# Small tiles in a pool of their own, and TensorE's dense operands at multiples of 256 bytes

## The chip, the cores and the metric

One core of a Trainium2 chip runs the whole program. The metric is the device time of one execution in microseconds, the median of several runs. TensorE multiplies, VectorE (DVE) and ScalarE (ACT) work on elements, GpSimd (POOL) does little here, and SyncE (SP) issues nearly all DMA transfers.

## The reference

Two layers of a decoder work on x of 1024 rows by 1024 columns, float32. Each layer does two things, and normalises the rows before and after each of them.

1. Mixing: h = norm(x) times a scale plus a shift, both from the condition vector c; one projection of h gives queries (8 heads of 64), keys and values (2 heads), and 512 columns u. Queries attend to the 128 last positions, with a sink for each head; u goes through trailing means of 2, 4, 8 and 16 rows and a small matrix for each group. The two results, 512 columns each, go through an output projection, are normalised, gated and added to x.
2. Feed-forward: f = (silu(h Wg) * (h Wu)) Wd with an inner width of 2816, then normalised, gated and added to x.

```
proj = h @ w_in + b_in;  q, k, v, u = split(proj)
x = x + gate_m * norm(concat(attention(q, k, v), pool(u)) @ w_out)
h = norm(x) * (1 + scale_f) + shift_f
x = x + gate_f * norm((silu(h @ w_gate) * (h @ w_up)) @ w_down)
```

## The kernel before

The 1024 rows are two halves of 512. To keep float32 accuracy every operand is split in two parts, hi and lo (`split`, lines 210 and 211: ScalarE rounds to float32r, VectorE subtracts), and every product is three matmuls (`mm3`, lines 236, 239 and 240): hi by hi, moving lo by stationary hi, moving hi by stationary lo, all into one PSUM bank. In the first argument after the destination stands the stationary operand, 128 columns; the other one moves, 512 columns in the dense stages, and each matmul loads its stationary operand anew.

The dense stages of each layer, in their order:
- `q_pass`, `kv_pass`, `u_pass`: the input projection. Weights come to `raw` tiles and are split into `hi` and `lo`; the activations stand split in `hT`. In the first two hT is stationary, in u_pass it moves. kv_pass moves 256 columns.
- `natural_proj`: the output projection; both operands are split into `hi` and `lo` tiles.
- `up_firsts`, `up_pair`: gate and up products, in seven products by a Strassen-like scheme (`double`, 8 groups of three matmuls for each right-hand operand into two banks). Stationary are weights in hi and lo; moving are `hT` in the first products and, after the region "up" is made, `t1`, `t2`, `t3`, `t4` and `b22`.
- `down`: seven products over 22 groups of inner columns. Stationary are activations in hi and lo; moving are weights in `bh`, with `ph` or `bl` for their low part, and in the last product `one_` and `two_` tiles.

Between the projections run the attention (scores with stationary `qT` and moving keys in `sa`; values with stationary `vz` and moving `pth` and `ph`; 256 columns each) and transposes, in which the identity `ident` moves and the transposed tile is stationary. Streams of work are Python generators that are stepped in turn, so the order of instructions is fixed by the code; the tile framework adds waits where tiles depend on each other. PSUM has four banks `acc` for dense products.

Memory: tiles lie in pools one behind the other, and `t_` takes a tile by its name from the pool that has it. The pool `const` begins at byte 16512 of each partition and holds 3840 bytes, with `ident` first; `sb` begins at 20352 and holds 126592 bytes, with small tiles (statistics, columns, rows, halos) between the large ones; the regions "mix", "up" and "down" follow at 146944, one after the other in the same place. In the trace the numbers at the end of tile names are left out: t stands for t1 to t4, b for b22, two_b and one_b for the tiles two_... and one_....

Addresses modulo 256 (of the first byte in a partition; slices of 128 or 512 columns begin at multiples of 512 bytes behind it):

| tiles | before |
|---|---|
| ident | 128 |
| raw, hi, lo, hT, fn, ar, sa, sb | 192 |
| G, ada, ph | 128 |
| t1 to t4, b22, bh, bl, one_, two_ | 0 |
| qT, vz, pth in layer 0 | 128 |
| qT, vz, pth in layer 1 | 0 |

Of the kernel before, what the change touches and what calls it, by code (L numbers as in the profile page):

```python
# [11 lines left out]
F32 = mybir.dt.float32  # L12
F32R = mybir.dt.float32r
# [7 lines left out]
P = 128  # L21
# [16 lines left out]
KD = D // P  # L38
# [27 lines left out]
def hybrid_decoder_kernel(  # L66
# [22 lines left out]
    nc = tc.nc  # L89

    const = ctx.enter_context(tc.tile_pool(name="const", bufs=1))
    sb = ctx.enter_context(tc.tile_pool(name="sb", bufs=1))
    ps = ctx.enter_context(tc.tile_pool(name="ps", bufs=1, space=PSUM))
    dr = ctx.enter_context(tc.tile_pool(name="dr", bufs=1, space=DRAM))


    SHARED = dict(
        hT=8, fn=4, raw=2, hi=3, lo=3, sa=2, sb=2, ar=2, ada=1, ph=3,
        junk=1, st=12, rs=8, ss=4, halo=8, G=1, rows=1, cols=2, colp=4, sk=2,
    )  # L100
    REGIONS = dict(
        mix=dict(cfa=2, cfb=2, qkv=6, bqkv=1, uT=4, pt=2, vz=5, rt=1, qT=1, pth=2, pwh=1, pwl=1),
        up=dict(t2=8, t1=8, t3=8, b22=8, t4=8),
# [8 lines left out]
            now.update(name=name, pool=tc.alloc_tile_pool(name=name, bufs=1, reuse_waits="tile"))  # L112

    def t_(tag, shape, dt=F32):
        if tag in SHARED:
            return sb.tile(shape, dt, tag=tag, name=tag, bufs=SHARED[tag])
        return now["pool"].tile(shape, dt, tag=tag, name=tag, bufs=REGIONS[now["name"]][tag])
# [3 lines left out]
    def part(tag, n=512):  # L121

        tile_, used = now.get(tag, (None, WIDE[tag]))
        if used + n > WIDE[tag]:
            tile_, used = t_(tag, [P, WIDE[tag]], F32 if tag == "raw" else F32R), 0
        now[tag] = (tile_, used + n)
        return tile_[:, used : used + n]
# [8 lines left out]


    eye = t_("G", [P, D])[:, :P]
    make_identity(nc, eye)
    ident_r = const.tile([P, P], F32R, name="ident")  # L140
    nc.vector.tensor_copy(ident_r, eye)
    ident = ident_r.bitcast(F32)
    ones = t_("pt", [P, P])
    nc.vector.memset(ones, 1.0)
    ones_r = const.tile([P, 1], F32R, name="ones_r")
    nc.vector.tensor_copy(ones_r, ones[:, 0:1])
    ones = ones_r.bitcast(F32)
    pick_row = t_("rt", [P, 7])
    nc.vector.memset(pick_row, 0.0)
    nc.vector.memset(pick_row[:, 3:4], 1.0)  # L150
    picks = const.tile([P, 7], F32R, name="picks")
    nc.vector.tensor_copy(picks, pick_row)

    mask = const.tile([P, 2, 2 * P], F32, name="mask")
# [18 lines left out]
    nc.vector.reciprocal(rcnt, rcnt)  # L173


    c_raw = const.tile([P, KD], F32, name="c_raw")
    nc.sync.dma_start(c_raw, c[0].rearrange("(p j) -> p j", j=KD))
    c_act = const.tile([P, KD], F32, name="c_act")
    nc.scalar.activation(c_act, c_raw, AF.Silu)


# [230 lines left out]
    def load_gate(l, sub):  # L412
        G = t_("G", [P, D])
        nc.sync.dma_start(G, gates[l, sub].to_broadcast([P, D]))
        return G
# [504 lines left out]
    def mix_out(l, cats, G):  # L920
        order = [*range(GRP, KD), *range(GRP)]
        left = [cats[k // 4][:, k % 4, :] for k in order]

        def wsrc(i, nh):
            k = order[i]
            cs = slice(nh * 512, (nh + 1) * 512)
            if k < GRP:
                return (
                    (slice(0, HD), None, w_out[l, k * HD : (k + 1) * HD, cs]),
                    (slice(HD, P), None, w_out[l, (GRP + k) * HD : (GRP + k + 1) * HD, cs]),  # L930
                )
            return ((ALLP, None, w_out[l, k * P : (k + 1) * P, cs]),)

        fn = [t_("fn", [P, D]) for _ in range(NT)]
        ss = t_("ss", [P, 8])
        return fn, ss, natural_proj(fn, left, wsrc, ss, G)
# [373 lines left out]
    for l in range(DEPTH):  # L1310
        cols = par["cols"]
# [37 lines left out]
        G = load_gate(l, 0)  # L1349
        fn, ss, out0 = mix_out(l, cats[0], G)  # L1350
# [23 lines left out]
        fn, ss, out1 = mix_out(l, cats[1], G)  # L1374
# [38 lines left out]
        G = load_gate(l, 1)  # L1413
# [3 lines left out]
        fn = [[t_(tag, [P, D]) for _ in range(NT)] for tag in ("fn",)]  # L1417
        fn.append([t_(tag, [P, D]) for tag in ("sa", "sa", "sb", "sb")])
        ss = [t_("ss", [P, 8]) for _ in range(NHALF)]
# [53 lines left out]
def build(arrays):  # L1473
    import concourse.bacc as _bacc

    nc = _bacc.Bacc("TRN2", target_bir_lowering=False, num_devices=1)
    args = []
    for name in _INS:
        a = arrays[f"in_{name}_dram"]
        args.append(  # L1480
            nc.dram_tensor(f"in_{name}_dram", a.shape, mybir.dt.from_np(a.dtype), kind="ExternalInput").ap()
        )
    for i, (shape, dtype) in enumerate(_OUTS):
        dt = mybir.dt.from_np(np.dtype(dtype))
        args.append(nc.dram_tensor(f"out_{i}_dram", shape, dt, kind="ExternalOutput").ap())
    with tile.TileContext(nc) as tc:
        hybrid_decoder_kernel(tc, *args)
    return nc
# [9 lines left out]
```

## Time and profile before

| | |
|---|---|
| median of 3 runs | 1985.68 us (1984.56 to 1991.52) |
| profiled execution | 1988.62 us |
| its span, first to last instruction | 1986.8 us |
| granted TensorE clock over the span | 0.988 |
| TensorE matmuls busy | 96%, 8958 instructions |
| weight loads busy | 78%, 8958 instructions |
| VectorE busy | 79%, 2907 instructions |
| ScalarE busy | 48%, 1794 instructions |
| GpSimd busy | 3%, 100 instructions |
| DMA | 336.62 MB, 169 GB/s over the span |

A busy time is the union of an engine's instructions. Matmuls are pipelined: one starts before the last one's end, so that how long one lasts in the rows is not how far it moves the next one; the starts in the timeline tell that.

### The profile page before, as it was taken

The numbers are of one execution on the slowest core, as the hardware profiler recorded it, in microseconds if no ns is written. First come the engines' busy times: TensorE is split into PE (matmuls) and PEld (weight loads), VectorE is DVE, ScalarE is ACT, GpSimd is POOL, SyncE is SP. The second block draws the span as 40 slices with busy tenths as digits, with TensorE's granted clock in tenths as the row PEclk, the third lists the DMA queues.
The fourth block names the chain that finished last, engine by engine and source line by source line (L and its number), as shares of the span: only waits on it lengthen the run. The fifth ranks groups of instructions, "written<-read, shape, count | busy, mean of one in ns | idle before, by whom it ended". The sixth has DMA issues, their size and how long they took to land. (4 is left out here: it accounts for less than half of the span.)

```text
span 1986.8 us, 26045 instructions
## 1 busy us (share of the span) xinstructions
PE 1898.7 (96%) x8958; PEld 1548.8 (78%) x8958; DVE 1566.9 (79%) x2907; ACT 957.0 (48%) x1794; POOL 50.3 (3%) x100
## 2 busy tenths in 40 slices
PE   7989989999999999999999899899999999999997
PEld 4777778877888887778887778788788788878886
DVE  6888975778888886877878889656887888667687
ACT  4775775662222223445648658745622222234452
POOL 1000000020000000000000000000200000000000
PEclk9999999999999999999999899999999999999999
DMA  9336554556455556833565455446555554474343
GB/s 325 87 118 191 184 167 133 174 181 198 162 169 175 165 165 243 280 123 101 169 201 174 128 149 186 137 129 191 170 185 175 188 174 157 153 259 156 112 138 106
DMA packets 222052, 336.62 MB, mean 169 GB/s; under 512 B 16696, under 2 KB 120008, under 8 KB 221920
## 3 DMA queue, kind: packets, MB, share of 16 engines
q1 hardware_dynamic: 221776, 334.92, 51.7%
q8 instruction: 70, 1.15, 0.2%
q14 instruction: 62, 0.51, 0.1%
q0 software_dynamic: 32, 0.00, 0.0%
q10 hardware_dynamic: 112, 0.04, 0.0%
HBM read 262.00 MB, written 72.89 MB: 169 GB/s over the span
## 5 line engine op out<-in xcount | busy, mean ns | idle before, releaser
L210 ACT ACTIVATE hi<-raw 128x1024 fp32r<-128x1024 f32 (+1 forms) x388 | 331.9, 867 | 341.1 <-PE acc L239 224.5
L211 DVE TENSOR_TENSOR lo<-raw,hi 128x1024 fp32r<-128x1024 f32 (+1 forms) x388 | 381.2, 988 | 82.5 <-ACT hi L210 82.2
L236 PE MATMUL acc<-t,hi 128*128 128x512 f32 x704 | 277.0, 393 | 5.1 <-ACT hi L210 5.1
L240 PE MATMUL acc<-t,lo 128*128 128x512 f32 x704 | 276.5, 394 | 5.0 <-DVE lo L211 5.0
L239 PE MATMUL acc<-t,hi 128*128 128x512 f32 x704 | 277.1, 394 | 0.0
L236 PE MATMUL acc<-bh,hi 128*128 128x512 f32 x528 | 205.5, 394 | 3.0 <-ACT bh L210 3.0
L240 PE MATMUL acc<-bh,lo 128*128 128x512 f32 x528 | 208.2, 394 | 0.0
L236 PE MATMUL acc<-hT,hi 128*128 128x512 f32 x480 | 192.0, 400 | 10.6 <-ACT hi L210 10.0
L1058 DVE TENSOR_TENSOR fn<-acc,fn 128x512 f32<-128x512 f32 x220 | 150.7, 685 | 53.1 <-PE acc L240 52.0
L239 PE MATMUL acc<-hT,hi 128*128 128x512 f32 x480 | 189.7, 395 | 0.0
L240 PE MATMUL acc<-hT,lo 128*128 128x512 f32 x480 | 188.2, 394 | 0.0
L240 PEld LDWEIGHTS acc<-t,lo 128*128 128x128 f32 x704 | 133.0, 189 | 36.9 <-DVE lo L211 7.9
L236 PEld LDWEIGHTS acc<-t,hi 128*128 128x128 f32 x704 | 132.9, 189 | 36.2 <-ACT hi L210 6.9
L239 PEld LDWEIGHTS acc<-t,hi 128*128 128x128 f32 x704 | 132.9, 189 | 28.9
L239 PE MATMUL acc<-ph,hi 128*128 128x512 f32 x320 | 127.4, 398 | 1.1 <-DVE ph L211 1.1
L236 PEld LDWEIGHTS acc<-bh,hi 128*128 128x128 f32 x528 | 99.1, 188 | 26.5 <-ACT bh L210 3.8
L270 DVE SCALAR_TENSOR_TENSOR ada<-ar,c_act,ada 128x512 f32<-128x512 f32 x140 | 104.6, 747 | 18.1 <-DMA ar<-in_ada_w_dram 16.8
L240 PEld LDWEIGHTS acc<-bh,lo 128*128 128x128 f32 x528 | 100.0, 189 | 22.6
L236 PEld LDWEIGHTS acc<-hT,hi 128*128 128x128 f32 x480 | 91.2, 190 | 30.5 <-ACT hi L210 11.4
L996 ACT ACTIVATE fn<-fn 128x512 f32<-128x512 f32 x44 | 27.9, 633 | 170.6 <-DVE fn L1058 170.6
L240 PEld LDWEIGHTS acc<-hT,lo 128*128 128x128 f32 x480 | 90.9, 190 | 18.8 <-DVE lo L211 0.4
L239 PEld LDWEIGHTS acc<-hT,hi 128*128 128x128 f32 x480 | 91.6, 191 | 17.6
(302 smaller groups left out, 3877.4 us busy)
## 6 DMA issues: line engine op xcount, KB each, us to landing
ar<-in_ada_w_dram SPq DMA_DIRECT2D x160, 256.0 KB
raw<-in_w_gate_dram SPq DMA_DIRECT2D x44, 512.0 KB
raw<-in_w_up_dram SPq DMA_DIRECT2D x44, 512.0 KB
raw<-in_w_in_dram SPq DMA_DIRECT2D x80, 256.0 KB
raw<-keeps SPq DMA_DIRECT2D x40, 512.0 KB
keeps<-fn SPq DMA_DIRECT2D x66, 256.0 KB
two_b<-in_w_down_dram SPq DMA_DIRECT2D x30, 512.0 KB
raw<-keepa SPq DMA_DIRECT2D x25, 512.0 KB
```

The source lines that it names most:

```text
L210: nc.scalar.activation(hi, src, AF.Copy)
L211: nc.vector.tensor_sub(lo, src, hi.bitcast(F32))
L236: ins = nc.tensor.matmul(dst, lh, rh, start=first, stop=False)
L239: nc.tensor.matmul(dst, lh, rl, start=False, stop=False)
L240: return nc.tensor.matmul(dst, ll, rh, start=False, stop=last)
L270: nc.vector.scalar_tensor_tensor(acc, w, c_act[:, i : i + 1], acc, op0=ALU.mult, op1=ALU.add)
L996: nc.scalar.activation(g, g, AF.Silu)
L1058: nc.vector.tensor_add(halves_of(dst)[m], bank, halves_of(src)[m])
```

## The change

The tiles of few bytes (junk, st, rs, ss, halo, rows, cols, colp, sk) leave the pool `sb` for a pool `small` that is opened before it. In `const` four small tiles are allocated ahead of `ident`. No operation, shape or buffer count is another.

```diff
     const = ctx.enter_context(tc.tile_pool(name="const", bufs=1))
+    small = ctx.enter_context(tc.tile_pool(name="small", bufs=1))
     sb = ctx.enter_context(tc.tile_pool(name="sb", bufs=1))
...
-    SHARED = dict(
-        hT=8, fn=4, raw=2, hi=3, lo=3, sa=2, sb=2, ar=2, ada=1, ph=3,
-        junk=1, st=12, rs=8, ss=4, halo=8, G=1, rows=1, cols=2, colp=4, sk=2,
-    )
+    SMALL = dict(junk=1, st=12, rs=8, ss=4, halo=8, rows=1, cols=2, colp=4, sk=2)
+    SHARED = dict(hT=8, fn=4, raw=2, hi=3, lo=3, sa=2, sb=2, ar=2, ada=1, ph=3, G=1)
...
     def t_(tag, shape, dt=F32):
+        if tag in SMALL:
+            return small.tile(shape, dt, tag=tag, name=tag, bufs=SMALL[tag])
         if tag in SHARED:
...
+    ones_r = const.tile([P, 1], F32R, name="ones_r")
+    picks = const.tile([P, 7], F32R, name="picks")
+    c_raw = const.tile([P, KD], F32, name="c_raw")
+    c_act = const.tile([P, KD], F32, name="c_act")
     ident_r = const.tile([P, P], F32R, name="ident")
...
-    ones_r = const.tile([P, 1], F32R, name="ones_r")
...
-    picks = const.tile([P, 7], F32R, name="picks")
...
-    c_raw = const.tile([P, KD], F32, name="c_raw")
...
-    c_act = const.tile([P, KD], F32, name="c_act")
```

By the sizes of the tiles `small` holds 3712 bytes from 20352 on, and `sb` begins at 24064 and holds 122880; the regions stay at 146944. `ident` moves from 16512 to 16640.

## Rows read from the trace of the kernel before

**Rows 1.** The page's head and its busy times: us (share of span) x instructions.

```profile
span 1986.8 us, 26045 instructions
...
PE 1898.7 (96%) x8958; PEld 1548.8 (78%) x8958; DVE 1566.9 (79%) x2907; ACT 957.0 (48%) x1794; POOL 50.3 (3%) x100
```

**Rows 2.** A stretch: us, busy time of each engine, granted clock, DMA share, GB/s.

```profile
500.00:700.00 200.00, 200.00 (x875) 163.57 (x874) 169.58 (x217) 53.08 (x61) 0.00 (x0) 1.00 0.51 169
```

**Rows 3.** TensorE's longest wait: us in total, times, longest us.

```profile
PE acc L236 <- ACT hi L210: 15.6, 11, 2.5
```

**Rows 4.** Timeline (start us, duration us), gate and up products, 40 steps.

```profile
1499.78 0.39 PE L236 MATMUL acc<-t,hi 128*128 128x512 f32 x1
...
1508.93 0.39 PE L239 MATMUL acc<-b,hi 128*128 128x512 f32 x1
```

**Rows 5.** Timeline, gate and up products with hT moving, 31 steps.

```profile
1687.72 0.39 PE L239 MATMUL acc<-hT,hi 128*128 128x512 f32 x1
...
1694.75 0.39 PE L240 MATMUL acc<-hT,lo 128*128 128x512 f32 x1
```

**Rows 6.** Timeline, output projection, 32 steps.

```profile
1314.71 0.39 PE L240 MATMUL acc<-hi,lo 128*128 128x512 f32 x1
...
1321.96 0.39 PE L239 MATMUL acc<-lo,hi 128*128 128x512 f32 x1
```

**Rows 7.** Timeline, down products, 32 steps.

```profile
1904.62 0.39 PE L240 MATMUL acc<-bh,lo 128*128 128x512 f32 x1
...
1911.97 0.39 PE L239 MATMUL acc<-bl,hi 128*128 128x512 f32 x1
```

**Rows 8.** Timeline, key and value projection, 256 columns, 22 steps.

```profile
1039.25 0.28 PE L236 MATMUL acc<-hi,hT 128*128 128x256 f32 x1
...
1041.89 0.28 PE L239 MATMUL acc<-lo,hT 128*128 128x256 f32 x1
```

**Rows 9.** Timeline, attention's values in layer 0, then the next matmul, 11 steps.

```profile
302.91 0.30 PE L239 MATMUL pv<-ph,vz 128*128 128x256 f32 x1
...
304.23 0.39 PE L239 MATMUL acc<-hT,hi 128*128 128x512 f32 x1
```

**Rows 10.** Timeline, attention's values in layer 1, then the next matmul, 11 steps.

```profile
1285.90 0.28 PE L239 MATMUL pv<-ph,vz 128*128 128x256 f32 x1
...
1287.20 0.39 PE L239 MATMUL acc<-hT,hi 128*128 128x512 f32 x1
```

**Rows 11.** Groups of TensorE by form: busy us, mean ns, idle before.

```profile
L236 PE MATMUL acc<-t,hi 128*128 128x512 f32 x704 | 277.0, 393 | 5.1 <-ACT hi L210 5.1
...
L236 PE MATMUL acc<-bh,hi 128*128 128x512 f32 x528 | 205.5, 394 | 3.0 <-ACT bh L210 3.0
...
L236 PE MATMUL acc<-hT,hi 128*128 128x512 f32 x480 | 192.0, 400 | 10.6 <-ACT hi L210 10.0 <-DVE fn L591 0.6
...
L236 PE MATMUL acc<-hi 128*128 128x512 f32 x256 | 100.4, 398 | 0.1
...
L236 PE MATMUL acc<-b,hi 128*128 128x512 f32 x176 | 68.9, 391 | 0.0
...
L236 PE MATMUL acc<-hi,hT 128*128 128x512 f32 x128 | 49.4, 405 | 4.9 <-DVE qkv L648 2.7 <-ACT hT L210 1.5 <-ACT hi L210 0.5
...
L236 PE MATMUL acc<-two_b,hi 128*128 128x512 f32 x80 | 31.5, 394 | 0.0
...
L236 PE MATMUL acc<-one_b,hi 128*128 128x512 f32 x8 | 3.3, 407 | 0.5 <-DVE sa L1136 0.5
```

**Rows 12.** Groups of VectorE by form.

```profile
L211 DVE TENSOR_TENSOR lo<-raw,hi 128x512 fp32r<-128x512 f32 x167 | 113.0, 684 | 14.4 <-ACT hi L210 14.3
...
L211 DVE TENSOR_TENSOR bl<-two_b,bh 128x512 fp32r<-128x512 f32 x40 | 27.4, 686 | 10.6 <-ACT bh L210 10.6
```

**Rows 13.** Groups of weight loads by form.

```profile
L239 PEld LDWEIGHTS acc<-t,hi 128*128 128x128 f32 x704 | 132.9, 189 | 28.9
...
L240 PEld LDWEIGHTS pv<-pth,vz 128*128 128x128 f32 x128 | 24.5, 191 | 0.3
```

## The prediction

> **What bounds the kernel now.** I read the first part of the page, then the stretches, the waits of TensorE, its timeline inside four stages, and last the groups by form. TensorE's matmuls are busy for 1898.7 of the 1986.8 us of the span [rows 1], so only 88 us hold no matmul. In the gate and up products of layer 0 the share is 200.00 of 200.00 us at a granted clock of 1.00, the 2.4 GHz level [rows 2]. The longest wait of TensorE, for ScalarE's split, sums to 15.6 us over the whole program [rows 3]. So for most of the span the time is a number of matmuls times the distance from one matmul's start to the next one's. The duration of a matmul in the rows (0.39 us) is a pipelined one and tells nothing here; the distance must be read from starts.
>
> At 2.4 GHz, 512 columns take 213.3 ns. The starts show more, and not the same everywhere:
> - Moving operand in t or b tiles (gate and up products): from 1499.78 to 1508.93 us there are 40 steps, 9.15 us, so 228.8 ns each [rows 4].
> - Moving operand hT, in the same function and the same stage, a few pairs later: from 1687.72 to 1694.75 us 31 steps, 7.03 us, 226.8 ns [rows 5].
> - Output projection, both operands from hi and lo: 1314.71 to 1321.96 us, 32 steps, 7.25 us, 226.6 ns [rows 6].
> - Down products, moving operand bh with ph or bl: 1904.62 to 1911.97 us, 32 steps, 7.35 us, 229.7 ns [rows 7].
>
> The addresses sort these four. By the sizes of the tiles in the pools, hi, lo and hT start at 192 modulo 256, the region's t, b22, bh and bl at 0, and ph at 128. Call that remainder the phase. Where both operands have phase 192, a step is 226.7 ns; where the stationary one has 192 and the moving one another phase, it is 228.8 to 229.7 ns. The pair in rows 4 and 5 differs in little but the phase of the moving operand, so I read the 2 ns as its effect.
>
> Matmuls of 256 columns say something on equal phases other than 192. Key and value projection, both at 192: 1039.25 to 1041.89 us, 22 steps, 120.0 ns [rows 8]. Values of the attention in layer 0, where all three tiles lie at 128: 302.91 to 304.23 us, 11 steps, 120.0 ns [rows 9]. The same in layer 1, where vz and pth lie at 0 and ph at 128: 1285.90 to 1287.20 us, 11 steps, 118.2 ns [rows 10]. 256 columns take 106.7 ns, so equal phases cost 13.3 ns over the columns at 128 and at 192 alike, and so they do at 512 columns (226.7 less 213.3 is 13.4 ns). That equal phases behave alike, whichever the phase is, is my main assumption: no row shows a 512-column matmul with both at 0.
>
> **The change part by part.** It adds, removes and moves no instruction; it moves tiles. The small tiles sum to 3712 bytes, and 20352 + 3712 = 24064 = 94 x 256, so every tile left in the sb pool gets phase 0; the sum of both pools is what sb was before, so the regions keep their addresses. No wait is added, and no queue gets another order.
>
> 1. *Gate and up products.* The stationary hi and lo go from 192 to 0; t and b22 are at 0 already. With equal phases a step goes from 228.8 to 226.7 ns. There are 704 + 176 groups of three matmuls [rows 11], 2640 matmuls, times 2.1 ns: -5.5 us.
> 2. *Down products.* Stationary 192 to 0, ph 128 to 0, the others stay at 0. (528 + 80 + 8) x 3 = 1848 matmuls [rows 11], times 229.7 - 226.7 = 3.0 ns: -5.5 us.
> 3. *Products with both operands at 192* (the first gate and up products, projections): both go to 0, equal before and after. (480 + 256 + 128) x 3 = 2592 matmuls [rows 11]: nothing. Bounds: 3.0 ns dearer, as rows 7 are against rows 6, is +7.8 us; cheaper by the 1.8 ns between rows 9 and 10 is -4.7 us.
> 4. *Matmuls of 256 columns.* In the scores the keys in sa go to 0 and qT stays at 128 or 0; the values in layer 0 get a ph at 0 beside tiles at 128. By the loops of the attention these are 40 in each of 16 blocks, 640 short matmuls, in stages where TensorE waits anyway. Bound: 1.8 ns either way, 1.1 us. I take +0.3 us.
> 5. *Identity.* It moves from 128 to 0 as the moving operand of transposes, whose stationary tiles mostly go from 192 to 0. 28 in each of the 16 blocks and four in each of 64 pieces of a normalised half make 704 transposes of 128 columns; by the same 1.8 ns either way 1.3 us. I take 0.
> 6. *VectorE and ScalarE.* Same work at other addresses. A subtraction of 512 columns takes 684 ns with operands at 192 (lo) and 686 ns with them at 0 (bl) [rows 12]. I take 0; 2 ns either way on the 207 subtractions of these two groups would be 0.4 us, beside TensorE's matmuls.
> 7. *Weight loads.* They last 189 ns with the stationary tile at 192 and 191 ns with vz at 128 or 0 [rows 13], inside the preceding matmul's step. I take 0.
> 8. *DMA.* Rows land at 0 instead of 192 in raw, ar, fn and hT. In the stretch of rows 2 the engines are busy for 0.51 of the time while TensorE never stops, so a faster landing has nothing to give there. I take 0.
>
> Sum of 1 to 5: -10.7 us. What is late next is the producers: VectorE is 170 of 200 us busy in the stretch of rows 2, and a step 1% shorter leaves it room. I let 0.3 us go to the waits of rows 3 and take -10.4 us. The profiled execution took 1988.62 us, 1.8 us more than its span and 2.9 us more than the median 1985.68. 1988.62 - 10.4 = 1978.2 us there; against the median 1975.3 us.
>
> A rule speaks against all of this. The Trainium skill, "SBUF — State Buffer", section "Who interferes with whom", says that TensorE has two independent read ports, one for the moving operand and one for the weights, and that it never waits on anyone; "TensorE: Matmul & The Clock Gate", section "Back-to-back issue gap", gives a warm step as N / 2.4 + 2.5 ns, 215.8 ns for 512 columns, whatever the addresses. By that the change gives nothing. The trace does not agree: no stage comes down to 215.8 ns, and rows 4 and 5 differ.
>
> **The rivals.**
> - *Phase is not the cause, or the gain is taken back.* The 2 ns between rows 4 and 5 could come from something else about the tiles, such as their number or the region they lie in, or the waits of rows 3 could grow by what the matmuls save. For it: two pairs of places are little evidence. Against it: rows 5 lie between matmuls of the kind of rows 4, in one stage. Time: 1985.7 us, give or take 3. This is also the case that the change doesn't do what it says.
> - *The start of the moving operand alone counts, and 192 is the good one.* Then what is at 0 stays as it is, and the 2592 matmuls of point 3 go from 226.7 to between 228.8 and 229.7 ns: +5.4 to +7.8 us, 1991 to 1993.5 us. Its place is the first gate and up products and the projections. For it: rows 4 to 7 allow it as well as they allow my reading. Against it: 128 and 192 cost the same in rows 8 and 9. It decides if the steps of rows 6 grow past 228 ns.
> - *The stationary operand's own start costs.* Nothing of 512 columns now has it at 0; layer 1 of the values has, and is 1.8 ns cheaper (rows 10 against 9). If all 7080 dense matmuls gained that on top, -12.7 us more: 1963 us. The far end is that the whole surplus over the columns goes, 13.4 ns x 7080 = -95 us beside the 11: 1880 us. Against the far end: rows 10 have both at 0 in two of three matmuls and still pay 11.5 ns over the columns.
>
> **How the numbers follow.** Forecast 0.50, no effect 0.22, moving operand alone 0.13, stationary operand 0.15. Predicted 1975.3 us; the likeliest case's own range is 1971 to 1981. For 8 in 10 I reach below 1963 toward the stationary case, to 1954, and above to 1991.5, which leaves out the upper half of the moving-operand case and the far end of the other. What can be told from no change is 0.5%, 9.9 us, so below 1975.8 counts as faster: six tenths of the forecast's 0.50 and nearly all of the stationary case's 0.15, with a little noise, 0.48. Slower is past 1995.6 us: the dearest end of the moving-operand case with the small costs of points 4 and 5 added, and collisions of engines that now all start rows at phase 0, together 0.12. Same 0.40.
>
> **What would show it.** Right: in the gate and up products and in the down products, 40 steps take 9.07 us instead of 9.15 and 9.19, and the output projection stays at 226.7 ns a step; busy time of the other engines' groups unchanged. Wrong: the stages keep their distances (first rival), the output projection gets longer (second), or every stage falls below 226 ns (third). It would also be wrong if the steps shorten as said and the span doesn't: then the waits of TensorE have grown by as much.

## The result, and the profile after

The changed kernel takes 1980.1 us (median of 18 runs); the kernel before, run beside it, takes 1989.18 us (median of 18). The ratio is 0.9949, with a 95% interval of 0.9938 to 0.9960: between 8 and 12 us less. Forecast was 0.9948 (1975.3 to 1985.68); the 1989 us of the larger sample put the predicted time 5 us below the measured one.

The page of the profiled execution after (answers to [rows 1]):

```profile
span 1977.8 us, 26045 instructions
...
PE 1891.2 (96%) x8958; PEld 1551.3 (78%) x8958; DVE 1564.9 (79%) x2907; ACT 957.1 (48%) x1794; POOL 49.7 (3%) x100
```

The span is 9.0 us shorter, the matmuls are busy for 7.5 us less, and the other engines do the same work. Three lines were added above `split` and `mm3`, so lines 236, 239 and 240 of before are 239, 242 and 243 now.

The stretch of [rows 2], 500 to 700 us, after the change (us, busy time and instructions of PE, PEld, DVE, ACT, POOL, granted clock, DMA share, GB/s):

```profile
500.00:700.00 200.00, 200.00 (x883) 164.83 (x883) 171.20 (x219) 53.05 (x60) 0.00 (x0) 1.00 0.50 170
```

TensorE is busy for the whole 200 us in both kernels at the same clock, but 883 matmuls lie in it, wholly or in part, where it was 875. 200 us through 883 is about 226.5 ns, through 875 about 228.6 ns.

The timeline after, in pairs of first and last start: 40 steps of the gate and up products ([rows 4]), 31 steps with hT moving ([rows 5], here in the input projection), 32 steps of the output projection ([rows 6]), and 32 steps of the down products ([rows 7]):

```profile
1438.73 0.39 PE L242 MATMUL acc<-t,hi 128*128 128x512 f32 x1
...
1447.80 0.39 PE L243 MATMUL acc<-b,lo 128*128 128x512 f32 x1
...
1285.49 0.39 PE L242 MATMUL acc<-hT,hi 128*128 128x512 f32 x1
...
1292.52 0.39 PE L243 MATMUL acc<-hT,lo 128*128 128x512 f32 x1
...
1310.42 0.39 PE L239 MATMUL acc<-hi 128*128 128x512 f32 x1
...
1317.68 0.39 PE L243 MATMUL acc<-hi,lo 128*128 128x512 f32 x1
...
1758.10 0.39 PE L243 MATMUL acc<-bh,lo 128*128 128x512 f32 x1
...
1765.36 0.39 PE L239 MATMUL acc<-bh,hi 128*128 128x512 f32 x1
```

The four distances are 9.07 us / 40, 7.03 / 31, 7.26 / 32 and 7.26 / 32: 226.8, 226.8, 226.9 and 226.9 ns, all one value within what two decimals can tell. Of before the first was 228.8 and the last 229.7; the two between have not changed. That is what the forecast asked for.

How long the two stages last is seen in the first and last start of their moving tiles, layer 0 and layer 1. In the kernel before (count, shortest/median/longest duration in ns, first to last start in us; first t, then bh):

```profile
L236 PE MATMUL acc<-t,hi x352: 388/392/628, 445.9 to 776.2; 128*128 128x512 f32 x176
...
L236 PE MATMUL acc<-t,hi x352: 388/392/628, 1429.8 to 1760.2; 128*128 128x512 f32 x176
...
L236 PE MATMUL acc<-bh,hi x264: 388/392/628, 778.5 to 972.1; 128*128 128x512 f32 x132
...
L236 PE MATMUL acc<-bh,hi x264: 388/392/505, 1762.5 to 1944.2; 128*128 128x512 f32 x132
```

After:

```profile
L239 PE MATMUL acc<-t,hi x352: 387/389/628, 449.3 to 775.9; 128*128 128x512 f32 x176
...
L239 PE MATMUL acc<-t,hi x352: 387/389/628, 1426.6 to 1754.0; 128*128 128x512 f32 x176
...
L239 PE MATMUL acc<-bh,hi x264: 388/389/628, 778.2 to 969.6; 128*128 128x512 f32 x132
...
L239 PE MATMUL acc<-bh,hi x264: 389/389/501, 1756.4 to 1935.4; 128*128 128x512 f32 x132
```

The t stretches go from 330.3 + 330.4 to 326.6 + 327.4 us, 6.7 us less; the bh stretches from 193.6 + 181.7 to 191.4 + 179.0, 4.9 us less. Of these 11.6 us, 9.0 arrive in the span of these two profiles: the first t starts 3.4 us later than before. Up to there the changed kernel and the kernels of experiments 3 to 7 have the same code at the same addresses, and in their profiles the first t starts anywhere from 445.7 to 449.9 us, so I take the 3.4 us as scatter of single executions.

### The profile page after: what moved, and what is told of

The parts are those of the page before. It is cut to its first block, busy times and chain, and to the rows that moved or that the text cites. A ratio compares the mean times of both kernels' runs of the same rounds, so it can differ in the third digit from the quotient of the medians.

```text
span 1977.8 us, 26045 instructions
## 1 busy us (share of the span) xinstructions
PE 1891.2 (96%) x8958; PEld 1551.3 (78%) x8958; DVE 1564.9 (79%) x2907; ACT 957.1 (48%) x1794; POOL 49.7 (3%) x100
```

## The experiments

In all of them but experiment 8 a tile is allocated that nothing uses, so that what follows it moves by some bytes. The diffs are shortened to what the edits do. "Difference" is the phase of the moving tiles less that of the stationary ones; it was 0 less 192, which is 64 modulo 256, in the gate and up products of the kernel before.

### 1. All dense operands at 64

```diff
# in the changed kernel
+    small.tile([P, 16], F32, tag="pad", name="pad", bufs=1)
     def t_(tag, shape, dt=F32):
```

> The changed kernel with one unused tile of 64 bytes at the end of the small pool, so that hi, lo, hT, ph and the regions' t, b22, bh, bl all begin at 64 modulo 256: equal phases, and no dense operand at a multiple of 256. Theory (what counts is the difference between the two operands' phases): steps of 226.7 ns in the gate and up products, the down products and the output projection, as in the changed kernel; ratio to the kernel before 0.993 to 0.997. Rival (multiples of 256 count in themselves): steps of 228.8 ns or more in every stage, ratio 0.999 or above.

Measured: 1980.65 us against 1989.77, ratio 0.9952 (0.9935 to 0.9969). Timeline, 40 steps of the gate and up products and 32 of the down products:

```profile
1444.96 0.39 PE L244 MATMUL acc<-t,hi 128*128 128x512 f32 x1
...
1454.03 0.39 PE L245 MATMUL acc<-t,lo 128*128 128x512 f32 x1
...
1766.45 0.39 PE L245 MATMUL acc<-bh,lo 128*128 128x512 f32 x1
...
1773.70 0.39 PE L244 MATMUL acc<-bl,hi 128*128 128x512 f32 x1
```

9.07 us / 40 and 7.25 / 32: 226.8 and 226.6 ns. The whole gain is there without one dense operand at a multiple of 256. What the change is named for is not what pays.

### 2. The regions moved instead, in the kernel before

```diff
             now.update(name=name, pool=tc.alloc_tile_pool(...))
+            if name in ("up", "down"):
+                now["pool"].tile([P, 48], F32, tag="pad", name="pad", bufs=1)
```

> The kernel before, its pools as they were, with an unused tile of 192 bytes at the start of the regions up and down: t, b22, bh, bl, one_ and two_ move from 0 to 192, where hi and lo are; ph stays at 128. No dense operand is at a multiple of 256. Theory (difference of phases): 226.7 ns a step in the gate and up products; in the down products the two matmuls of three that move bh, and those that move bl, come down to about 227, those that move ph stay near 229; together 8 to 10 us, ratio 0.995 to 0.9965. Rival (multiples of 256): no step shorter than in the kernel before, ratio 0.999 to 1.003.

Measured: 1982.59 us, ratio 0.9956 (0.9940 to 0.9972), in the expected range. 40 steps of the gate and up products, then 41 of the down products in three parts:

```profile
1441.64 0.39 PE L242 MATMUL acc<-t,hi 128*128 128x512 f32 x1
...
1450.70 0.39 PE L245 MATMUL acc<-b,hi 128*128 128x512 f32 x1
...
1762.61 0.39 PE L245 MATMUL acc<-ph,hi 128*128 128x512 f32 x1
...
1766.73 0.40 PE L245 MATMUL acc<-bl,hi 128*128 128x512 f32 x1
...
1768.58 0.39 PE L242 MATMUL acc<-bh,hi 128*128 128x512 f32 x1
...
1771.98 0.39 PE L242 MATMUL acc<-bh,hi 128*128 128x512 f32 x1
```

9.06 us / 40 is 226.5 ns: the gate and up products have the gain, with all operands at 192. In the down products groups of three matmuls with ph and groups with bl come in turn, several of a kind in a row. The first 18 steps shown belong to groups with ph: 4.12 us, 228.9 ns each. Here the expectation missed: two matmuls of three have equal phases there and should have come to 227, but all three stand at 228 to 230 ns. One odd tile, ph at 128, is enough to keep the whole group long. Then come groups with bl, in which every tile lies at 192. Their first eight steps still take 1.85 us, 231 ns each; the next 15 take 3.40 us, 226.7 ns each, as expected. So the odd tile also lengthens matmuls just after its last use, but not the whole stage.

### 3. The same difference as before, at other addresses

```diff
# in the changed kernel, the tile of experiment 2 with 64 bytes
+                now["pool"].tile([P, 16], F32, tag="pad", name="pad", bufs=1)
```

> The changed kernel with an unused tile of 64 bytes at the start of the regions up and down: the stationary hi and lo and the moving hT and ph stay at 0, t, b22, bh, bl, one_ and two_ go to 64. The difference moving less stationary is 64, as in the kernel before (0 less 192), the addresses are others. Theory (difference of phases): 228.8 ns a step in the gate and up products again, 229 to 230 in the down products, the output projection stays at 226.7; ratio to the kernel before 0.999 to 1.001. Rival (the stationary operand's own start at a multiple of 256 is what pays): steps stay at 226.7 to 227.5 ns, ratio 0.994 to 0.997.

Measured: 1991.51 us, ratio 1.0010 (0.9998 to 1.0022): the gain is gone. 40 steps of the gate and up products, 32 of the output projection, 32 of the down products:

```profile
1439.54 0.39 PE L248 MATMUL acc<-t,hi 128*128 128x512 f32 x1
...
1448.69 0.39 PE L249 MATMUL acc<-t,lo 128*128 128x512 f32 x1
...
1312.31 0.39 PE L248 MATMUL acc<-lo,hi 128*128 128x512 f32 x1
...
1319.56 0.39 PE L245 MATMUL acc<-hi 128*128 128x512 f32 x1
...
1773.53 0.39 PE L245 MATMUL acc<-bh,hi 128*128 128x512 f32 x1
...
1780.95 0.39 PE L249 MATMUL acc<-bh,lo 128*128 128x512 f32 x1
```

9.15 us / 40 is 228.8 ns, the very distance of [rows 4], although the stationary operand lies at 0 now and the moving one at 64. The output projection, which the edit doesn't touch, keeps 226.6 ns. The down products, with bh and bl at 64 and ph at 0, are at 7.42 / 32 = 231.9 ns, dearer than the 229 to 230 expected. These 32 steps mix two kinds of groups. By the starts in the trace, groups with bl, whose moving tiles all lie at 64, settle at 229 ns a step; groups with ph, which lies at 0 like the stationary tiles, settle at 233. So a tile that agrees with the stationary operand, but not with the other moving tile, makes its group dearer here.

### 4 to 7. Eight differences

The edit is that of experiment 3 with another number of bytes in each layer.

```diff
+                now["pool"].tile([P, n // 4], F32, tag="pad", name="pad", bufs=1)   # n: by layer
```

> The changed kernel with the regions up and down of layer 0 shifted by 32 bytes and those of layer 1 by 128 bytes, hi and lo at 0: two more differences of phase in one run, read from the steps of each layer. Theory (difference of phases, 0 the best seen): both layers' gate and up products above 226.7 ns, by up to 3 ns. Rival (only misalignment to 64 or 128 bytes costs): layer 1 at 226.7 ns, layer 0 above. If a difference other than 0 gave less than 226.7 ns, 0 would not be the best.

> The changed kernel with the regions up and down shifted by 256 bytes in layer 0 and by 192 in layer 1, hi and lo at 0. Theory (difference of the two starts modulo 256): layer 0 stays at 226.8 ns a step in the gate and up products; layer 1 at 229 or above. Rival (the period is longer, 512 bytes or more, and the change equalised that): layer 0 above 228 ns.

> The changed kernel with the regions up and down shifted by 288 bytes in layer 0 and by 96 in layer 1. Theory (difference modulo 256): layer 0 behaves as a shift of 32, 233.3 ns a step in the gate and up products as in the run with 32; layer 1 above 228 ns. Rival (longer period): layer 0 differs from 233.3 ns by more than 1 ns.

> The changed kernel with the regions up and down shifted by 224 bytes in layer 0 and by 160 in layer 1: the last two differences in steps of 32 bytes. Theory (0 is the best difference): both above 228 ns a step in the gate and up products. Rival (some difference beats 0): one of them below 226.5 ns, which would make a faster kernel.

One execution each, 2000.12, 1995.03, 2001.64 and 2000.22 us, beside 1987 to 1990 for the kernel before. What counts are 40 steps of the gate and up products in layer 0 and in layer 1. Shifts of 32 and 128:

```profile
460.34 0.40 PE L249 MATMUL acc<-t,lo 128*128 128x512 f32 x1
...
469.67 0.40 PE L245 MATMUL acc<-b,hi 128*128 128x512 f32 x1
...
1476.37 0.40 PE L248 MATMUL acc<-t,hi 128*128 128x512 f32 x1
...
1485.70 0.40 PE L249 MATMUL acc<-t,lo 128*128 128x512 f32 x1
```

256 and 192:

```profile
463.17 0.39 PE L245 MATMUL acc<-t,hi 128*128 128x512 f32 x1
...
472.24 0.39 PE L248 MATMUL acc<-b,hi 128*128 128x512 f32 x1
...
1440.20 0.40 PE L248 MATMUL acc<-t,hi 128*128 128x512 f32 x1
...
1449.53 0.40 PE L249 MATMUL acc<-t,lo 128*128 128x512 f32 x1
```

288 and 96:

```profile
460.54 0.40 PE L249 MATMUL acc<-t,lo 128*128 128x512 f32 x1
...
469.87 0.40 PE L245 MATMUL acc<-b,hi 128*128 128x512 f32 x1
...
1581.86 0.39 PE L248 MATMUL acc<-t,hi 128*128 128x512 f32 x1
...
1591.19 0.40 PE L248 MATMUL acc<-t,hi 128*128 128x512 f32 x1
```

224 and 160:

```profile
460.55 0.40 PE L248 MATMUL acc<-t,hi 128*128 128x512 f32 x1
...
469.88 0.40 PE L249 MATMUL acc<-b,lo 128*128 128x512 f32 x1
...
1445.74 0.40 PE L249 MATMUL acc<-t,lo 128*128 128x512 f32 x1
...
1455.11 0.39 PE L245 MATMUL acc<-b,hi 128*128 128x512 f32 x1
```

| difference | kernel, layer | 40 steps, us | one step, ns |
|---|---|---|---|
| 0 | changed kernel; experiments 1, 2 | 9.07 (2: 9.06) | 226.8 (2: 226.5) |
| 32 | experiment 4, layer 0 | 9.33 | 233.3 |
| 64 | before; experiment 3 | 9.15 | 228.8 |
| 96 | experiment 6, layer 1 | 9.33 | 233.3 |
| 128 | experiment 4, layer 1 | 9.33 | 233.3 |
| 160 | experiment 7, layer 1 | 9.37 | 234.3 |
| 192 | experiment 5, layer 1 | 9.33 | 233.3 |
| 224 | experiment 7, layer 0 | 9.33 | 233.3 |
| 256 | experiment 5, layer 0 | 9.07 | 226.8 |
| 288 | experiment 6, layer 0 | 9.33 | 233.3 |

256 is as good as 0 and 288 as bad as 32, so 256 bytes is a period in these two cases. No difference in steps of 32 bytes beats 0, so none of them gives a faster kernel. Experiment 4's expectation held in its direction and not in its size: it allowed up to 3 ns above 226.7, and 6.6 came. And the kernel before was by chance at the mildest of the bad differences: by an estimate from the table, any other multiple of 32 that isn't one of 256 would have cost it 4.5 to 5.5 ns more in each of 2640 matmuls, 12 to 15 us.

### 8. The identity alone

```diff
# in the kernel before
+    ones_r, picks, c_raw, c_act allocated here, as in the changed kernel
     ident_r = const.tile([P, P], F32R, name="ident")
```

> One part of the change alone: the kernel before with the four small tiles allocated ahead of the identity, so that it lies at a multiple of 256; all pools as before. Theory (the identity moves in transposes only, 704 short ones in stages that wait anyway): ratio 0.999 to 1.001 to the kernel before. Rival (the identity carries part of the gain): 0.998 or below.

Measured: 1986.86 us against 1987.56, ratio 0.9999 (0.9988 to 1.0010). The identity's address is worth nothing that can be measured.

### 9. One of the stationary tiles off

```diff
# in the changed kernel
+    lop = ctx.enter_context(tc.tile_pool(name="lop", bufs=1))
+    lop.tile([P, 8], F32, tag="pad", name="pad", bufs=1)
...
+        if tag == "lo":
+            return lop.tile(shape, dt, tag=tag, name=tag, bufs=SHARED[tag])
```

The regions up and down are shifted as well, by 224 bytes in layer 0.

> The changed kernel with the three lo tiles in a pool of their own behind sb, 32 bytes off a multiple of 256; hi stays at 0. In layer 0 the regions up and down are shifted back to 0, in layer 1 they lie at 32. So in the gate and up products one of the three matmuls of a group has a stationary operand (lo) 32 bytes off the moving one in layer 0, and the other two (hi) in layer 1. Where all three differ by 32 the step is 233.3 ns, where none does 226.8. Theory A (a matmul is slowed by its own stationary operand's difference): layer 0 about 229 ns in the mean, with the third matmul of a group, which uses lo, the long one; layer 1 about 231, with the first two long. Theory B (a matmul is slowed by the load of the next stationary operand, which goes on while it runs): the same means, but in layer 0 the second matmul of a group is the long one, during which lo is loaded; in layer 1 the first and the third. Rival (the difference of phases between pairs is not what counts): both layers at 226.8 or both at 233.3.

Measured: one execution, 2013.08 us beside 1989.55; lo is off in the projections too, so those are slower as well. Seven starts in a row in layer 0; L249, L252 and L253 are the first, second and third matmul of a group, and only the third has lo as its stationary operand:

```profile
599.63 0.40 PE L249 MATMUL acc<-t,hi 128*128 128x512 f32 x1
599.86 0.40 PE L252 MATMUL acc<-t,hi 128*128 128x512 f32 x1
600.10 0.39 PE L253 MATMUL acc<-t,lo 128*128 128x512 f32 x1
600.33 0.40 PE L249 MATMUL acc<-t,hi 128*128 128x512 f32 x1
600.56 0.40 PE L252 MATMUL acc<-t,hi 128*128 128x512 f32 x1
600.80 0.39 PE L253 MATMUL acc<-t,lo 128*128 128x512 f32 x1
601.03 0.40 PE L249 MATMUL acc<-t,hi 128*128 128x512 f32 x1
```

From first to first it is 0.70 us, two groups in 1.40: 233.3 ns a matmul in the mean, the full price of a difference of 32, though only one matmul of three has it. The second matmul is the long one (0.24 us to the next start, twice, against 0.23): that is where theory B put it, since lo is loaded while it runs. Over the whole stage in layer 0 the starts in the trace give 232.4, 238.7 and 228.4 ns for the first, second and third matmul. But neither theory gave the mean, and the value that I had named for the rival, 233.3 ns, is what came. In layer 1, where hi was off and lo was not, 30 steps take 7.00 us, and the mean is the same:

```profile
1500.39 0.40 PE L249 MATMUL acc<-t,hi 128*128 128x512 f32 x1
...
1507.39 0.40 PE L249 MATMUL acc<-t,hi 128*128 128x512 f32 x1
```

There the three take 235.5, 233.4 and 230.8 ns: the first two are the long ones, as in theory A. So the price is not paid matmul by matmul: it falls on matmuls whose own operands agree as well. Nor is it one price for a whole stream with an odd tile. In experiment 2 ph's difference is 192 (128 less 192, modulo 256). It costs 6.6 ns a step where all moving tiles have it (experiment 5), but ph's groups pay 2.2 ns a step. How large the price of a mixed group is, no rule here says. What holds in every stretch read is that matmuls of 512 columns come down to 226.7 ns in the mean only where all tiles in use have one phase.

## Why the prediction was right

The forecast's mechanism held and so did its size, for the two terms that carry it.

- *Gate and up products* (point 1): forecast 228.8 to 226.7 ns and -5.5 us; measured 226.8 ns and -6.7 us in the t stretches, which hold some matmuls of hT and some stops too. The steps alone, about 2800 that follow without a stop, are 2.0 ns shorter in the mean, 5.7 us.
- *Down products* (point 2): forecast 229.7 to 226.7 ns and -5.5 us; measured 226.9 ns and -4.9 us in the bh stretches, which leave out the last of the seven products.
- *Equal before, equal after* (point 3): the assumption that equal phases behave alike at any phase had no row of 512 columns with both operands at 0. The output projection kept its distance at 0, and experiment 1 showed it at 64, experiment 2 at 192.
- *Identity* (point 5): 0 forecast, 0.9999 measured. *Short matmuls* (point 4): +0.3 us forecast; no run's time separates it, but the starts in the traces of before and after do. Where they follow without a stop (less than 135 ns apart), the scores go from 117.7 to 119.6 ns in layer 0 and from 116.9 to 118.0 in layer 1, the values from 118.8 to 118.2 and from 118.0 to 119.1: by an estimate from these means and their 640 matmuls, +0.5 us. The other runs with the same differences there agree within 0.4 ns.
- *Waits* (the 0.3 us given back): not told apart from the scatter of single executions.

Those 256-column matmuls don't follow the rule of the 512-column ones. The values have all their tiles at one phase in layer 0 before and in layer 1 after, and there they are 0.6 and 1.1 ns longer than with ph apart. The prediction read 1.8 ns between rows 9 and 10; the 11 steps of rows 9 hold one of 132 ns, and over all the values of the two layers it is 0.8 ns (118.8 and 118.0). It used the 1.8 ns for bounds and for the third rival, not for the forecast's own terms.

The rivals fell. *Phase is not the cause*: experiments 1 to 3 switch the gain on and off by addresses alone. *The moving operand's start alone*: it would have lengthened the output projection with both operands at 0, and it did not. *The stationary operand's own start*: in experiment 3 it stays at 0 and the gain is gone, and no stage fell below 226 ns. The rule weighed in the prediction, of the Trainium skill, "SBUF — State Buffer", section "Who interferes with whom", is that TensorE's two read ports are independent and TensorE waits for no one. By it the change would have given nothing; the steps here run from 226.8 to 234.3 ns by addresses alone.

One thing in the working was wrong without harm here. I priced the effect by the pair of operands of one matmul. Experiments 2 and 9 show that one tile of another phase also slows the matmuls around it that don't use it. In the down products that makes ph's move from 128 to 0, which I had listed in passing, a condition for most of the term of -5.5 us: in experiment 2, which leaves ph out, groups with ph keep 228.9 ns, and the bh stretches, 192.5 + 181.0 us, are 1.8 us shorter than before instead of 4.9.

What stays open is the mechanism below. The place of the long step in layer 0 of experiment 9 would fit a collision between the running matmul's reads and the load of the next stationary operand, but layer 1 of the same run was not as that theory had it, and no run measured the reads themselves. Shown is that the addresses set the step; why they do is not.

## What to carry to other kernels

Where a long stream of float32r matmuls of 512 columns reloads the stationary operand each time, put all its tiles, moving and stationary, at one address modulo 256. Which one doesn't matter (0, 64 and 192 gave the same), and a pool of odd-sized small tiles ahead of them, or one tile with another phase, is enough to lose 1 to 3% of a step. For matmuls of 256 columns no gain was seen. Measure it by starts, not durations: over 32 or 40 steps two decimals of a timeline show a nanosecond. When a change says what it does by an absolute rule (multiples of 256), try the same relation at other addresses before believing the rule.

## What the runs showed of the hardware that was not expected

- The price is not graded by the difference: 32, 96, 128, 192 and 224 bytes all give 233.3 ns, 160 gives 234.3, and 64 gives 228.8, less than half of the others' surplus over 226.8.
- A difference of 32 in one matmul of three costs as much as in all three (233.3 ns in experiment 9 as in experiment 4). A difference of 192 in one of three costs a third of what it costs in all three (228.9 ns in experiment 2, 233.3 in experiment 5).
- A change of phase in the stream is felt for some steps: in experiment 2 the eight steps after the last use of ph take 231 ns each before 226.7 ns is reached.
- At one phase 512 columns take 226.7 ns and 256 columns 120.0 ns [rows 8], at a granted clock of 1.00. The difference, 106.7 ns for 256 columns, is one column in each cycle of 2.4 GHz, so by this estimate both pay 13.3 ns, 32 cycles, on top of their columns. At 512 columns no address tried takes any of it away; the values and scores, of 256 columns, lie a little lower, at 116.9 to 119.6 ns in the mean.
